# Split forms of the inner activations in 14 pieces between the product groups of the next up tiles

## Chip, cores and metric

The kernel runs on one core of one Trainium2 chip. The metric is the device time of one execution in microseconds (us), lower is better; every time below comes from runs of the kernel before or from the trace of one profiled execution of it.

## What is computed

The reference is one layer of a decoder trunk: four token mixers in parallel, an output projection, and a SwiGLU feed-forward block. The change touches the feed-forward block alone:

```python
h2 = layer_norm(x) * (1.0 + sc2) + sh2
up_a, up_b = jnp.split(h2 @ p['w_ffn_up'], 2, axis=-1)
ffn = (jax.nn.silu(up_a) * up_b) @ p['w_ffn_down']
x = layer_norm(ALPHA_DN * x + (1.0 + g2) * ffn, p['ln2_g'], p['ln2_b'])
```

There are 1056 tokens (1024 of the prompt, 32 of the samples), a model width of 1024 and an inner width of 2816, which is 22 tiles of 128. The inner activations are `silu(up_a) * up_b`.

## The kernel before

Tokens stand in three blocks of 352 (`TB`), the halves of a block are 176 wide (`HB`). Each matrix product is made in float16 from high and low halves, three matmuls for each product of 128 by 128 (`mm3`, L89).

**Seven products.** Most of the feed-forward block is computed by the scheme with seven products in place of eight (`seven`, L1655). Each tile of it is computed in two parts: a wide one of two blocks (matmuls of 352 columns) and a narrow one of one block (176 columns); `SUBS` lists them. So a tile has 14 product groups, in the order of `ORDER7` (L1653); a group is 12 matmuls for an up tile and 9 for a down tile. Products 0, 2, 3 and 5 are summed in the same PSUM bank, one after the other. After 0, 2 and 3 ScalarE (ACT) copies the bank's running sum out (L1683, to the tiles `ct`, `cu` or `af`), and TensorE (PE) can't begin product 2 before the copy after 0 is done, nor 3 before the copy after 2, nor 5 before the copy after 3. Products 1 and 6 share a second bank, product 4 has its own (`x7`). VectorE (DVE) adds the others (L1680). Below, "the copy after product 2" is the one of the wide part unless the narrow one is named, and "the work between" is what PE's order holds between the last matmul of product 2 and the first of product 3 of the wide part.

**Up tiles.** `up` makes one tile of inner activations, `af`, from h2: seven products, then tanh on ACT (L1854) and three steps on DVE (L1855, L1857). Tiles come in pairs; `ups(i)` makes tiles 2i and 2i+1. Pairs 0 and 1 are computed directly (L1820 to L1834), pairs 2 to 10 by seven products.

**Split forms.** Before a pair can be an input of the down projection, `forms(i)` makes seven combinations of its four quarters, each split in a high and a low half, in a slot of `ring` (3 slots, L1841). For each of the two parts there are 4 subtractions on DVE (L1869, in place in `af`), 7 high halves on ACT (L108) and 7 low halves on DVE (L116). A low half waits for its high half, a combined form for its subtraction.

**The order.** The loop at L1921 to L1934 is: forms 0, forms 1, up pair 2; forms 2, up pair 3; down chunk 0 (4 tiles, which read three slots); forms 3, up pair 4; forms 4, up pair 5; forms 5, up pair 6; down chunk 1; and again three pairs and down chunk 2. The tile framework puts the instructions of each engine into an order of its own: an instruction of a higher priority stream goes first where it is ready in the framework's model of time. `self.sup` (evacuations and weights) stands before `self.br` (the forms), which stands before `self.lo` (matmuls). Each engine's queue is then fixed and runs in order.

**Weights.** For each tile `pair_weights` (L1613) loads two blocks of weights by DMA (queue of SyncE), scales them on ACT (L1622), makes five sums on GpSimd (POOL: L1635 to L1643) and splits seven forms, high half on ACT (L1630), low half on POOL (L1631). The high and low halves are the tiles `whl` and `wf`.

## Time and profile before

| What | us |
|---|---|
| median of 3 runs | 1918.86 |
| lowest and highest run | 1918.74, 1921.48 |
| profiled execution, its own time | 1927.88 |
| its span, from the first to the last instruction | 1925.8 |
| PE busy, share of the span | 1734.6, 90% |
| DVE busy | 1297.0, 67% |
| ACT busy | 970.8, 50% |
| POOL busy | 953.9, 50% |

The seven-product part of the feed-forward block runs from 1282 to about 1840 us of the span. The profiled execution took 9.0 us longer than the median, so a difference worked out from its trace is carried over to the median as a difference. 2.1 us of its time lie outside the span.

### The profile page before, as it was taken

How to read it: one execution, taken by the hardware profiler on the slowest of the kernel's cores; microseconds unless marked ns; L12 is line 12 of the kernel's file. 1: busy time of each engine (PE TensorE's matmuls, PEld its weight loads, DVE VectorE, ACT ScalarE, POOL GpSimd, SP SyncE). 2: the span in 40 equal slices, each digit the busy share in tenths (PEclk: the TensorE clock that was granted, in tenths of full speed). 3: DMA queues.
4: the chain of work that ended last, by engine and by line, in shares of the span. 5: the costliest groups of instructions: out<-in, count | busy, mean ns of one | idle time of the engine just before them, and what ended most of it. 6: DMA issues, size and time to landing. Idle time of an engine off the chain costs nothing.

```text
span 1925.8 us, 36541 instructions
## 1 busy us (share of the span) xinstructions
PE 1734.6 (90%) x14985; PEld 1198.5 (62%) x14985; DVE 1297.0 (67%) x2161; ACT 970.8 (50%) x1796; POOL 953.9 (50%) x952
## 2 busy tenths in 40 slices
PE   7899999999899998788689899988999998999896
PEld 3466666656566665556367555556666776767675
DVE  6763777668676765386986479677467657755748
ACT  3642454465554645235664665645445644554434
POOL 1826421222354444744541553278577667675733
PEclk9999999999999999889799999989999999999999
DMA  8222220122311112313232340001121112111112
GB/s 310 75 90 64 73 59 23 49 58 54 96 50 58 62 40 98 73 41 102 77 110 77 129 137 1 1 23 44 48 64 56 48 44 65 56 37 53 50 28 91
DMA packets 63615, 130.60 MB, mean 68 GB/s; under 512 B 16408, under 2 KB 35928, under 8 KB 63192
## 3 DMA queue, kind: packets, MB, share of 16 engines
q1 hardware_dynamic: 61912, 124.07, 20.8%
q0 software_dynamic: 1536, 4.20, 0.7%
q8 instruction: 117, 1.92, 0.4%
q14 instruction: 50, 0.41, 0.1%
HBM read 117.36 MB, written 10.88 MB: 67 GB/s over the span
## 4 chain that ended last, share of the span: by engine, by line
PE 35%; DVE 26%; POOL 12%; ACT 10%; DMA 9%; issue 7%; SPq 1%; another core or an unknown queue 0%; ACTq 0%; DVEq 0%; POOLq 0%
PE gps L87 25%; DMA wraw<-in_w_up 3%; POOL wf L1631 2%; DVE x L1903 2%; POOL whl L1631 2%; DVE ring L116 2%; PE nps L87 1%; DMA wraw<-in_w_down 1%; DVE af L1869 1%; ACT wraw L1622 1%; DVE dacc L758 1%; POOL wraw L1635 1%; PE dp L87 1%; POOL wraw L1638 1%; POOL wraw L1639 1%
## 5 line engine op out<-in xcount | busy, mean ns | idle before, releaser
L87 PEld LDWEIGHTS <-whl 128*128 128x128 f16 x6992 | 623.5, 100 | 386.1 <-issue 74.9
L87 PE MATMUL gps<-h,whl 128*128 128x352 f16 (+1 forms) x4344 | 692.9, 314 | 49.0 <-ACT ct L1683 14.8
L87 PEld LDWEIGHTS <-wf 128*128 128x128 f16 x2232 | 197.7, 99 | 71.6 <-issue 13.8
L1631 POOL TENSOR_TENSOR wf<-wraw,wf 128x512 f16<-128x512 f32 (+1 forms) x102 | 122.8, 1206 | 145.8 <-ACT wf L1630 142.9
L1631 POOL TENSOR_TENSOR whl<-wraw,whl 128x512 f16<-128x512 f32 (+1 forms) x136 | 169.2, 1250 | 47.0 <-ACT whl L1630 46.8
L114 POOL TENSOR_TENSOR whl<-wraw,whl 128x1024 f16<-128x1024 f32 (+1 forms) x66 | 149.1, 2260 | 81.2 <-ACT whl L108 79.2
L105 ACT ACTIVATE wraw<-wraw 128x1024 f32<-128x1024 f32 (+2 forms) x96 | 96.4, 1005 | 127.4 <-DMA wraw<-in_w_gate 40.1
L87 PE MATMUL gps<-tf,whl 128*128 128x352 f16 (+1 forms) x1152 | 141.1, 280 | 18.6 <-ACT ct L1683 6.9
L1622 ACT ACTIVATE wraw<-wraw 128x1024 f32<-128x1024 f32 (+1 forms) x68 | 66.5, 978 | 111.0 <-DMA wraw<-in_w_up 62.2
L1630 ACT ACTIVATE whl<-wraw 128x512 f16<-128x512 f32 (+1 forms) x136 | 79.9, 589 | 78.8 <-POOL wraw L1635 34.5
L87 PE MATMUL gps<-ring,whl 128*128 128x352 f16 (+1 forms) x864 | 103.8, 276 | 13.1 <-DVE x L1903 13.1
L87 PE MATMUL gps<-y,wbr 128*128 128x352 f16 x576 | 105.4, 319 | 8.1 <-DVE gth L1771 3.8
L1680 DVE TENSOR_TENSOR ct<-ct,gps 128x352 f32<-128x352 f32 (+1 forms) x84 | 35.4, 424 | 106.5 <-PE gps L87 90.5
L1523 POOL TENSOR_TENSOR mix<-mix,gth 128x352 f32<-128x352 f32 x48 | 54.0, 1125 | 98.0 <-DVE gth L1494 87.1
L87 PE MATMUL gps<-mix,wo 128*128 128x352 f16 x576 | 88.8, 315 | 5.7 <-DVE gth L1771 3.4
L116 DVE TENSOR_TENSOR ring<-af,ring 128x352 f16<-128x352 f32 (+2 forms) x134 | 82.0, 645 | 7.8 <-ACT ring L108 7.7
L108 ACT ACTIVATE whl<-wraw 128x1024 f16<-128x1024 f32 (+1 forms) x82 | 84.8, 1035 | 4.4 <-DMA wraw<-in_w_ada 3.5
L87 PE MATMUL gps<-h,wf 128*128 128x352 f16 (+1 forms) x624 | 79.4, 283 | 6.6 <-DVE gth L1494 5.5
L87 PEld LDWEIGHTS <-wbr 128*128 128x128 f16 x576 | 56.5, 99 | 39.2 <-issue 10.2
L87 PEld LDWEIGHTS <-wo 128*128 128x128 f16 x576 | 56.7, 99 | 38.6 <-issue 5.9
L108 ACT ACTIVATE ring<-af 128x352 f16<-128x352 f32 (+2 forms) x134 | 52.2, 427 | 46.4 <-DVE af L1869 30.4
L87 PE MATMUL gps<-tf,wf 128*128 128x352 f16 (+1 forms) x528 | 66.6, 283 | 3.8 <-ACT cu L1683 3.6
(625 smaller groups left out, 3381.4 us busy)
## 6 DMA issues: line engine op xcount, KB each, us to landing
wraw<-in_w_up SPq DMA_DIRECT2D x44, 512.0 KB, 3.5
wraw<-in_w_gate SPq DMA_DIRECT2D x32, 512.0 KB, 3.9
wraw<-in_w_ada SPq DMA_DIRECT2D x32, 512.0 KB, 3.5
wraw<-in_w_in SPq DMA_DIRECT2D x20, 512.0 KB, 4.0
wraw<-in_w_down SPq DMA_DIRECT2D x24, 384.0 KB, 3.1
x<-in_xT SPq DMA_DIRECT2D x12, 704.0 KB, 7.7
araw<-in_w_ada SPq DMA_DIRECT2D x16, 512.0 KB, 10.9
wraw<-in_w_branch SPq DMA_DIRECT2D x8, 512.0 KB, 3.5
```

The source lines that it names most:

```text
L87: self.nc.tensor.matmul(out, lhsT=lhsT, rhs=rhs, start=start, stop=stop, skip_group_check=resume)
L105: nc.scalar.activation(src, src, AF.Copy, scale=scale)
L108: nc.scalar.activation(hi, src, AF.Copy, scale=scale)
L114: nc.gpsimd.tensor_tensor(lo, src, hi, op=ALU.subtract)
L116: nc.vector.tensor_tensor(lo, src, hi, op=ALU.subtract)
L758: nc.vector.scalar_tensor_tensor(acc[:, :L], ext[:, k:k + L], wts[:, i, k:k + 1], acc[:, :L], op0=ALU.mult, op1=ALU.add)
L1523: nc.gpsimd.tensor_tensor(o, o, g, op=ALU.add)
L1622: nc.scalar.activation(raw, raw, AF.Copy, scale=SW)
L1630: nc.scalar.activation(hi, src, AF.Copy)
L1631: nc.gpsimd.tensor_tensor(lo, src, hi, op=ALU.subtract)
L1680: add = lambda o, p: nc.vector.tensor_tensor(o, o, p, op=ALU.add)
L1903: nc.vector.scalar_tensor_tensor(x[:, h, z], part(h, z), gate[:, m, 0:1], x[:, h, z], op0=ALU.mult, op1=ALU.add)
```

## The change

`forms` no longer issues its instructions itself. It returns the slot and a generator with 14 steps (7 forms for the wide part, then 7 for the narrow one); each step is one form: its subtraction, where it has one, the high half and the low half. The order of the forms becomes 0, 1, 6, 3, 2, 4, 5. `seven` takes one step after each product group, while a generator is set, inside `issue_after(self.dve)`: each DVE instruction of the step is queued behind the DVE instruction noted last (an add, or the last step of an evacuation). ACT instructions of the step get no such edge. Only the last forms made before a pair are handed to it: forms 1 to pair 2, 2 to 3, and so on up to forms 8 to pair 9; forms 0 is made at once, as before. After the 14 groups of a pair's first tile all steps are taken.

```diff
+            def add(o, p):
+                self.dve = nc.vector.tensor_tensor(o, o, p, op=ALU.add).ins
...
+            if self.side is not None:
+                with self.tc.issue_after(self.dve):
+                    next(self.side, None)
...
-            for b, nb in self.SUBS:
...
-                with self.br:
-                    put(0, x1)
-                    sub(x1, x2, x1)
-                    put(1, x1)
-                    sub(x2, y2, x2)
-                    put(6, y2)
-                    sub(x1, y2, x1)
-                    put(2, x1)
-                    put(3, x2)
-                    put(4, y1)
-                    sub(y1, y1, x1)
-                    put(5, y1)
-            return R
+            def make():
+                for b, nb in self.SUBS:
...
+                    for f, src, p, q in ((0, x1, None, None), (1, x1, x2, x1), (6, y2, None, None), (3, x2, y2, x2),
+                                         (2, x1, y2, x1), (4, y1, None, None), (5, y1, y1, x1)):
+                        with self.br:
+                            if p is not None:
+                                sub(src, p, q)
+                            put(f, src)
+                        yield
+
+            return R, make()
...
-        def ups(i):
+        def ups(i, side=None):
+            self.side = side
             for t in (2 * i, 2 * i + 1):
                 w = self.full_forms()
                 self.pair_weights([I["w_up"][2 * t + j] for j in range(2)], 4, w)
                 up(t, w)
-
-
-        rs = [forms(i) for i in range(NSK // 2)]
+            for _ in self.side or ():
+                pass
+            self.side = None
+
+
+        rs = []
+        for i in range(NSK // 2):
+            R, side = forms(i)
+            rs.append(R)
+            if i < NSK // 2 - 1:
+                for _ in side:
+                    pass
         ahead = NSK // 2
-        ups(ahead)
+        ups(ahead, side)
```

No engine gets more or fewer instructions: DVE has 2163 in its order before and after, ACT 1798, PE 28936 (matmuls and weight loads). The order changes from the first forms on. Line numbers behind the edits shift: L1683 becomes L1685, L1869 becomes L1878, L1903 becomes L1908.

DVE, first tile of pair 4, right after the last down tile of chunk 0. Of before (`ring` is a low half, L1869 a subtraction, `x_13853` and `mod` belong to the down tile's evacuation, and the last row is the add of product 4, narrow part):

```order
L116 TENSOR_TENSOR ring<-af_14268,ring 128x352 x3
L116 TENSOR_TENSOR ring<-af_14268,ring 128x176
L1898 TENSOR_TENSOR ct<-ct,mod 128x32
L1903 SCALAR_TENSOR_TENSOR x_13853<-ct,mod,x_13853 128x144
L116 TENSOR_TENSOR ring<-af_14268,ring 128x176 x2
L1869 TENSOR_TENSOR af_14268<-af_14268 128x352
L1869 TENSOR_TENSOR af_14268<-af_14268 128x176
L1907 TENSOR_TENSOR x_13853<-x_13853,ct 128x32
L1869 TENSOR_TENSOR af_14268<-af_14268 128x352
```

The same place in the changed kernel:

```order
L116 TENSOR_TENSOR ring<-af_14268,ring 128x352 x3
L1903 TENSOR_TENSOR ct<-ct,mod 128x32
L1908 SCALAR_TENSOR_TENSOR x_13853<-ct,mod,x_13853 128x144
L1878 TENSOR_TENSOR af_14268<-af_14268 128x352
L1912 TENSOR_TENSOR x_13853<-x_13853,ct 128x32
L1878 TENSOR_TENSOR af_14268<-af_14268 128x352
L116 TENSOR_TENSOR ring<-af_14268,ring 128x352
L1878 TENSOR_TENSOR af_14268<-af_14268 128x352
L116 TENSOR_TENSOR ring<-af_14268,ring 128x352
L1681 TENSOR_TENSOR ct<-ct,x_16875 128x176
```

The narrow part's low halves, three of them, no longer stand ahead of the first wide subtraction; the narrow part as a whole comes later.

ACT at the same place. Of before (`wraw`, `whl` and `wf` are weights; the two `ct` rows are the copies after product 2, wide and narrow):

```order
L1622 ACTIVATE wraw<-wraw 128x1024
L1630 ACTIVATE wf<-wraw 128x512
L1630 ACTIVATE whl<-wraw 128x512
L108 ACTIVATE ring<-af_14268 128x352
L108 ACTIVATE ring<-af_14268 128x176
L1683 ACTIVATE ct<-gps 128x352
```

In the changed kernel:

```order
L1622 ACTIVATE wraw<-wraw 128x1024
L1630 ACTIVATE wf<-wraw 128x512
L1630 ACTIVATE whl<-wraw 128x512
L108 ACTIVATE ring<-af_14268 128x352
L1685 ACTIVATE ct<-gps 128x352
L108 ACTIVATE ring<-af_14268 128x352
```

One high half, not two, stands between the weights and the copy after product 2.

ACT, second tile of pair 5, from the narrow copy after product 0 to the wide copy after product 2. Of before:

```order
L1683 ACTIVATE ct<-gps 128x176
L108 ACTIVATE ring<-af_14268 128x352
L1630 ACTIVATE wf<-wraw 128x512
L108 ACTIVATE ring<-af_14268 128x176
L108 ACTIVATE ring<-af_14268 128x352
L1622 ACTIVATE wraw<-wraw 128x1024
L108 ACTIVATE ring<-af_14268 128x176
L1683 ACTIVATE ct<-gps 128x352
```

In the changed kernel:

```order
L1685 ACTIVATE ct<-gps 128x176
L108 ACTIVATE ring<-af_14268 128x352
L108 ACTIVATE ring<-af_14268 128x176
L108 ACTIVATE ring<-af 128x176
L1630 ACTIVATE wf<-wraw 128x512
L1622 ACTIVATE wraw<-wraw 128x1024
L1685 ACTIVATE ct<-gps 128x352
```

The high halves of subtracted forms of the next forms (the second `128x352` and the second `128x176`) are gone from there; the last narrow piece of forms 4 has come in.

The framework also places the matmuls of product 4 otherwise. PE's order between products 2 and 3 of the wide part holds, beside the 12 narrow matmuls of product 2, these matmuls of product 4 (narrow and wide):

| tile | before | changed |
|---|---|---|
| pair 3, first | 11 narrow, 12 wide, 4 wide of the next product 0 | 12 narrow, 7 wide |
| pair 3, second | 12 narrow, 9 wide | 10 narrow, 5 wide |
| pair 4, first | 7 narrow, 12 wide, 2 of the next product 0 | 12 narrow, 8 wide |
| pair 4, second | 12 narrow, 12 wide | 9 narrow, 12 wide, 1 of the next product 0 |
| pair 5, first | 12 narrow, 9 wide | 12 narrow, 3 wide |
| pair 5, second | 12 narrow, 12 wide | 12 narrow, 4 wide |
| pair 6, first | 12 narrow, 5 wide | 12 narrow, 12 wide |
| pair 7, first | 8 narrow, 12 wide | 12 narrow, 8 wide |
| pair 7, second | 12 narrow, 9 wide | 9 narrow, 12 wide, 1 of the next product 0 |
| pair 8, first | 12 narrow, 12 wide, 3 of the next product 0 | 12 narrow, 3 wide |
| pair 8, second | 12 narrow, 11 wide | 12 narrow, 4 wide |

The rest of them stand behind product 3 in both kernels. At the end of down chunk 0, ACT's order in the changed kernel has the scaling of weights L1622 ahead of the wide copy after product 3 of the last down tile; before, it stood behind it. In the first tile of pair 9, the weights' high half `whl` (L1630) that stood ahead of the wide copy after product 3 (to `cu`) now stands behind it.

## Rows read from the trace of the kernel before

**Rows 1.** The page, part 1: busy time of the engines.
```profile
PE 1734.6 (90%) x14985; PEld 1198.5 (62%) x14985; DVE 1297.0 (67%) x2161; ACT 970.8 (50%) x1796; POOL 953.9 (50%) x952
```
**Rows 2.** Waits of PE, 1280 to 1840 us: total, times, longest.
```profile
PE gps L87 <- ACT ct L1683: 21.7, 14, 5.8
PE gps L87 <- DVE x L1903: 16.6, 12, 1.9
PE gps L87 <- POOL whl L1631: 4.9, 2, 4.4
PE gps L87 <- ACT cu L1683: 4.2, 4, 1.9
```
**Rows 3.** PE in order of time, pairs 2 and 3: start, length, [idle before].
```profile
1295.26 3.68 PE L87 MATMUL gps<-tf,whl 128*128 128x352 f16 x12 [5.77 <-ACT ct L1683]
...
1307.60 3.24 PE L87 MATMUL gps<-h,whl 128*128 128x352 f16 x12 [3.12 <-ACT ct L1683]
...
1317.17 3.81 PE L87 MATMUL gps<-tf,whl 128*128 128x352 f16 x17 [4.44 <-POOL whl L1631]
1320.82 1.95 PE L87 MATMUL gps<-tf,wf 128*128 128x352 f16 x12
1322.61 0.31 PE L87 MATMUL gps<-h,wf 128*128 128x352 f16 x1
...
1352.86 4.58 PE L87 MATMUL gps<-h,whl 128*128 128x352 f16 x39 [1.88 <-ACT ct L1683]
...
1359.12 2.86 PE L87 MATMUL gps<-tf,wf 128*128 128x352 f16 x24 [1.68 <-ACT cu L1683]
```
**Rows 4.** PE in order of time, boundary after chunk 0, pairs 4 and 5.
```profile
1443.22 4.21 PE L87 MATMUL gps<-ring,wf 128*128 128x352 f16 x36
...
1458.62 4.73 PE L87 MATMUL gps<-h,whl 128*128 128x352 f16 x39 [1.43 <-ACT ct L1683]
...
1479.00 4.88 PE L87 MATMUL gps<-h,whl 128*128 128x352 f16 x39 [1.62 <-ACT ct L1683]
...
1497.84 2.86 PE L87 MATMUL gps<-h,whl 128*128 128x352 f16 x24 [0.23 <-ACT ct L1683]
...
1518.62 4.88 PE L87 MATMUL gps<-h,whl 128*128 128x352 f16 x39 [1.27 <-ACT ct L1683]
```
**Rows 5.** Busy time in a window of pair 2: length, PE, PEld, DVE, ACT, POOL, clock, DMA.
```profile
1305.00:1310.00 5.00, 2.40 (x9) 1.26 (x9) 5.00 (x14) 2.77 (x8) 0.43 (x2) 0.68 0.24 97
```
**Rows 6.** ACT in order of time, around the copies of pairs 4 and 5.
```profile
1457.48 0.74 ACT L108 ACTIVATE ring<-af 128x352 f16<-128x352 f32 x2 [3.69 <-DVE af L1869]
1458.13 0.44 ACT L1683 ACTIVATE ct<-gps 128x352 f32<-128x352 f32 x1
...
1516.54 0.50 ACT L108 ACTIVATE ring<-af 128x352 f16<-128x352 f32 x1 [2.58 <-DVE af L1869]
...
1518.13 0.44 ACT L1683 ACTIVATE ct<-gps 128x352 f32<-128x352 f32 x1
```
**Rows 7.** DVE in order of time: low halves in pair 2 and in pair 4.
```profile
1302.75 3.48 DVE L116 TENSOR_TENSOR ring<-af,ring 128x352 f16<-128x352 f32 x4
...
1452.57 3.56 DVE L116 TENSOR_TENSOR ring<-af,ring 128x352 f16<-128x352 f32 x4
```
**Rows 8.** Groups of the wide forms on DVE, by form, 1100 us to the end.
```profile
L116 DVE TENSOR_TENSOR ring<-af,ring 128x352 f16<-128x352 f32 x67 | 49.2, 743 | 6.1 <-ACT ring L108 6.1
L1869 DVE TENSOR_TENSOR af<-af 128x352 f32<-128x352 f32 x36 | 24.2, 684 | 0.1
```
**Rows 9.** POOL: one low half of weights in order of time, and its group on the page.
```profile
1309.91 7.21 POOL L1631 TENSOR_TENSOR whl<-wraw,whl 128x512 f16<-128x512 f32 x1 [4.57 <-ACT whl L1630]
...
L1631 POOL TENSOR_TENSOR whl<-wraw,whl 128x512 f16<-128x512 f32 (+1 forms) x136 | 169.2, 1250 | 47.0 <-ACT whl L1630 46.8
```
**Rows 10.** ACT in order of time at the end of down chunk 0.
```profile
1441.30 0.46 ACT L1683 ACTIVATE af<-gps 128x352 f32<-128x352 f32 x1 [1.60 <-PE gps L87]
1443.36 1.06 ACT L1622 ACTIVATE wraw<-wraw 128x1024 f32<-128x1024 f32 x1 [1.60 <-POOL wraw L1635]
```

More of the change, by code (lines that the diff above doesn't have):

```diff
@@ L1679, in seven @@
             c11, c12, c22 = c[i][0][:, 0], c[i][0][:, 1], c[i][1][:, c[i][1].shape[1] - 1]
-            add = lambda o, p: nc.vector.tensor_tensor(o, o, p, op=ALU.add)
+            def add(o, p):
+                self.dve = nc.vector.tensor_tensor(o, o, p, op=ALU.add).ins
             with self.sup:
@@ L1832, in ffn @@
                     nc.vector.scalar_tensor_tensor(o, o, 1.0, va, op0=ALU.add, op1=ALU.mult)
-                    nc.vector.scalar_tensor_tensor(o, o, c2, vb, op0=ALU.mult, op1=ALU.mult)
+                    self.dve = nc.vector.scalar_tensor_tensor(o, o, c2, vb, op0=ALU.mult, op1=ALU.mult).ins
             self.place7(h2, b, self.t3[b])
@@ L1856, in evac @@
                 for h in range(2):
-                    nc.vector.scalar_tensor_tensor(d[:, h], d[:, h], c2, other[b][h], op0=ALU.mult, op1=ALU.mult)
+                    self.dve = nc.vector.scalar_tensor_tensor(d[:, h], d[:, h], c2, other[b][h],
+                                                              op0=ALU.mult, op1=ALU.mult).ins
             self.seven(w, 4, xu, self.SUBS, evac, ct)
@@ L1864, in forms @@
             X, Y = af[2 * i], af[2 * i + 1]
-            for b, nb in self.SUBS:
-                c = slice(b * HB, (b + nb) * HB)
-                x1, x2, y1, y2 = X[:, 0, c], X[:, 1, c], Y[:, 0, c], Y[:, 1, c]
-                put = lambda f, src: self.split(R[:, f, 0, c], R[:, f, 1, c], src)
-                sub = lambda o, p, q: nc.vector.tensor_tensor(o, p, q, op=ALU.subtract)
-                with self.br:
-                    put(0, x1)
-                    sub(x1, x2, x1)
-                    put(1, x1)
-                    sub(x2, y2, x2)
-                    put(6, y2)
-                    sub(x1, y2, x1)
-                    put(2, x1)
-                    put(3, x2)
-                    put(4, y1)
-                    sub(y1, y1, x1)
-                    put(5, y1)
-            return R
+            def make():
+                for b, nb in self.SUBS:
+                    c = slice(b * HB, (b + nb) * HB)
+                    x1, x2, y1, y2 = X[:, 0, c], X[:, 1, c], Y[:, 0, c], Y[:, 1, c]
+                    put = lambda f, src: self.split(R[:, f, 0, c], R[:, f, 1, c], src)
+                    sub = lambda o, p, q: nc.vector.tensor_tensor(o, p, q, op=ALU.subtract)
+                    for f, src, p, q in ((0, x1, None, None), (1, x1, x2, x1), (6, y2, None, None), (3, x2, y2, x2),
[6 more added lines that the diff above has]
+            return R, make()
         gate = self.mod[:, 40:48]
@@ L1918, in ups @@
                 up(t, w)
-        rs = [forms(i) for i in range(NSK // 2)]
+            for _ in self.side or ():
[8 more added lines that the diff above has]
+                    pass
         ahead = NSK // 2
-        ups(ahead)
+        ups(ahead, side)
         for c in range(3):
             while len(rs) < 3:
-                rs.append(forms(ahead))
+                R, side = forms(ahead)
+                rs.append(R)
                 ahead += 1
-                ups(ahead)
+                ups(ahead, side)
             for mp in range(KD // 2):
@@ L2006, in build @@
     B.wraw_bufs, B.whl_bufs = 3, 4
+    B.side = None
     B.consts()
```

## Prediction

> **What bounds the kernel.** I read the page's busy times first. PE is busy for 1734.6 of 1925.8 us, DVE 67%, ACT and POOL 50% [rows 1], so time can only come from PE's idle time or from its clock. I then read PE's waits between 1280 and 1840 us, the only part in which the order changes [rows 2]. The reader is to see four releasers there. ACT's copies `ct` hold PE for 21.7 us in 14 waits, the copies `cu` for 4.2, a low half of weights on POOL for 4.9, and the down tiles' L1903 on DVE for 16.6. The last is an evacuation that the change does not touch. At most 21.7 + 4.2 + 4.9 = 30.8 us are within the change's reach.
>
> PE in order of time shows where they are. Pair 2 has the three long ones, 5.77, 3.12 and 4.44 [rows 3]; pairs 3 to 5 have some of 0.23 to 1.88 [rows 3, 4]; the other seven `ct` waits, in pairs 3 and 5 to 8, add 21.7 less the seven shown there (5.77, 3.12, 1.88, 1.43, 1.62, 0.23, 1.27), 6.4 us, about 0.9 each. After the long waits the clock was down as well: 12 wide matmuls took 3.24 us behind the wait of 3.12, and 12 of them later run in 1.95 [rows 3]; the granted clock in that window was 0.68, a mean of the two levels of 1.2 and 2.4 GHz [rows 5]. From the starts 1320.82 and 1322.61 a wide matmul at full clock is 1.79/12 = 0.149 us [rows 3], and I take a narrow one, with half the columns, at half of it, 0.075.
>
> **Why the copies are late.** PE cannot begin product 3 before ACT's copy after product 2. ACT is not busy then; it waits, in its order, behind a high half whose subtraction DVE has not reached. At 1457.48 ACT had waited 3.69 us for a subtraction, and the copy followed at 1458.13; at 1516.54 it had waited 2.58 us [rows 6]. DVE meanwhile was working off low halves: four in 3.56 us at 1452.57 [rows 7]. A wide low half costs 0.743 us and a wide subtraction 0.684 on the mean of its group [rows 8]. The change does not shorten these. It alters what stands ahead of the copies and how much of product 4 PE has to do until they come.
>
> **Pair 2.** Up to its first forms nothing moves, and the high halves ahead of the first copy are those of forms 0, made at once as before: 5.77 stays. For the wait of 3.12, two of the four low halves in the row of 3.48 us [rows 7] go behind a subtraction, which is worth 0 to 1.7 us (3.48/2) to the copy. I take 0.8, the middle, since most of forms 1 still lies dense there in DVE's order. The wait of 4.44 is for one low half of weights on POOL that took 7.21 us where its group has a mean of 1.25 [rows 9], while DVE was busy for all 5.00 us of the window and its 14 instructions [rows 5]. Its worth is 0 to 4.44; I take half, 2.2, because the spread takes part of DVE's work out of the 7 us but not all of it. This is a cause read from one coincidence of rows. The Trainium skill (SBUF — State Buffer, Who interferes with whom) says that a DVE instruction with two SBUF inputs contends with a GpSimd instruction that reads SBUF, and that who issues first holds the shared pair of ports for one whole instruction. By that rule POOL would be let in after the DVE instruction that it met; the row's 7.21 is longer than one such instruction, so rule and row do not fit unless the lock is lost again and again, and by the rule alone nothing would be gained at this place: the sum would be 2.2 and 0.5 (its clock) less, and the time about 1916.
>
> With shorter waits, half of the slow matmuls behind these two come back: (3.24 − 1.95)/2 = 0.6 behind the first, and for 17 at the second (3.81 − 17 × 0.149 = 1.3)/2, rounded down to 0.5. Bounds are 0 and 2.6. Pair 2: −0.8 − 2.2 − 1.1 = **−4.1**.
>
> **First tiles of pairs 3 to 9.** With one narrow high half fewer ahead of the copy and the first wide subtraction one low half earlier (3.56/4 = 0.9 [rows 7]), the copy comes some 1.1 us earlier; the high half I take at 0.2, below the 0.37 of one in the row of 0.74 x2 [rows 6], as two overlap. Against that PE has less to do until then, by the table of product 4. In pair 4: (5 × 0.075) − (4 + 2) × 0.149 = −0.5, so −1.1 + 0.5 = −0.6. In pair 7: less work by 0.3, −0.8. In pair 3 less work by 1.3 (9 wide fewer, one narrow more) eats the 1.1: 0; the wait of 1.68 for `cu` [rows 3] has the same L1622 ahead of it in both orders and stays. In pair 5, 0.9 less work (6 wide) on a wait of 0.23 [rows 4]: 0. Pair 6 has 1.0 more work but little wait: 0. Pair 8 has 1.8 less work where its wait is of another product: I add +0.4, between 0 and 1.8 − 1.1 = 0.7. In pair 9 the longest `cu` wait, 1.9 [rows 2], stands behind a weight split that waits for POOL and now follows the copy: −1.5, between 0 and −1.9. First tiles: **−2.5**.
>
> **Second tiles.** There the subtracted forms of the next pair leave the place ahead of the copy. That removes at least the 0.50 high half, at most the wait of 2.58 as well [rows 6]; the copy cannot come before product 2 ends and L1622 still stands there, so I take 0.6, near the lower end. Work between is less by 0.75 in pair 3, 8 × 0.149 = 1.2 in pair 5 and 1.05 in pair 8: 3.0 − 3 × 0.6 = +1.2. In pair 4, where 1.62 stands [rows 4], it is nearly unchanged: −0.5. In pair 7 it is 0.37 more: −1.0. Second tiles: **−0.3**.
>
> **Boundary after chunk 0.** ACT's L1622 now stands ahead of the wide copy after product 3. It waited for POOL until 1443.36 and took 1.06; the copy was made at 1441.30 before [rows 10]. PE goes on to the product behind that copy at 1443.22 without a wait [rows 4]. If L1622 lands when it did, the copy ends at 1443.36 + 1.06 + 0.46 = 1444.9, 1.7 after PE's need, less the 6 matmuls of the next tile (some 0.4 to 0.9 us at either width) that PE can take in between: **+1.3**, between 0 (L1622 earlier) and 1.7.
>
> **DMA and counts.** No instruction is added and no DMA moves to another queue, so there is no term there; SP's order matters only through L1622, priced above.
>
> **Sum.** −4.1 − 2.5 − 0.3 + 1.3 = −5.6 us against the profiled execution's 1927.88, which gives 1922.3. That execution was 9.0 above the median of 1918.86; carried over as a difference, the forecast is **1913.3**.
>
> **Rivals.**
>
> *Slower: PE runs out of work.* The copies come no earlier, since ACT queues behind whichever high half waits for DVE, while product 4 has moved behind product 3. Then each us of work lost lengthens a wait that is there already: 1.3 + 0.75 (pair 3), 0.5 (4), 0.9 + 1.2 (5), 0.3 (7), 1.05 (8) = 6.0, and 1.3 at the boundary: +7.3, 1926. It decides where copies come earlier by less than about 0.8 us. For it speaks that every late copy of [rows 6] has DVE as its releaser and that DVE's total is unchanged; against it that fewer low halves precede the subtractions.
>
> *No change.* Gains and losses of 1 us cancel, or POOL's 7.21 stays (−3.4 + 0.5 of clock, about −3 in all), or the change does less than it says: the edges bind DVE alone, the framework hoists ACT's high halves as before, and the orders differ little in pair 2. Sums from −3.8 to +3.8; 1918 as its middle.
>
> *All waits on copies go.* The `ct` waits without the first are 15.9, `cu` 4.2, POOL 4.9, clock 2.4: 27.4 us. Three quarters of it would be −20, 1899. For it speaks that ACT is idle for half of the span; against it that forms 1 stays dense in pair 2 and that PE has less work between.
>
> **How the numbers follow.** A difference of 0.2%, 3.8 us, is about what a measurement of this kernel can tell from no change. Forecast (−3.8 to −14) 0.38, all waits gone 0.08, no change 0.32, slower 0.22. Faster is 0.38 + 0.08 = 0.46. The forecast's own range follows from the bounds of its terms: 1905 to 1915. The whole range leaves out half of the slower case's tail beyond its price and most of the large gain: 1903 to 1926.
>
> **What would show it.** In the trace after: the wait of 5.77 unchanged, that of 3.12 near 2.3, the POOL row at 4 to 5 us in place of 7.21; `ct` waits at 16 to 18 in place of 21.7; L1903's waits still near 16.6; in pairs 5 and 8 the second tile's wait grown by 0.4 to 0.6; a new wait of about 1.3 before the product behind `af` at the end of chunk 0. The forecast is wrong if `ct` waits grow beyond 21.7 (then PE ran out of work), if POOL's long row stays and the time still falls (then it came from copies), or if new waits arise in the down tiles.

## The result, and the profile after

The changed kernel takes 1930.23 us at the median (21 runs, 1921.37 to 1936.32), the kernel before 1918.86 (21 runs, 1914.25 to 1921.91): 11.4 us slower, a ratio of 1.0059 with a 95% interval of 1.0046 to 1.0071. The forecast was 1913.3 in a range of 1903 to 1926.

The two profiled executions alone would not tell this. Their spans are 1925.8 and 1925.3 us: that of before lay 9.0 us above its median, that of the changed kernel (1927.24) 3.0 below. Up to the first long wait of PE both orders are the same, and there the changed kernel was already 10.5 us ahead (the wait begins at 1279.00, [rows 3] 1289.49). So the profiles have to be laid over each other at that wait. A second profile of the program before exists (the first run below, "without the edge"). From the product ahead of that wait to the last up pair, busy time by windows of that profile, and then of the changed kernel (length; PE, PEld, DVE, ACT, POOL busy; clock; DMA):

```profile
1277.50:1819.80 542.30, 494.52 (x4284) 373.92 (x4283) 356.77 (x638) 279.76 (x603) 382.45 (x325) 0.98 0.17 52
```

```profile
1274.10:1828.90 554.80, 499.60 (x4282) 375.88 (x4280) 378.77 (x638) 281.86 (x602) 375.62 (x325) 0.98 0.17 51
```

The same work takes 12.5 us longer; against the first profile of before, laid over at the same marks (543.60 us), it is 11.2. Of the 12.5, 5.1 are PE's own busy time (499.60 − 494.52). PE has the same matmuls, so that is clock: by windows of 5 us, length times the share missing from the full granted clock adds up to 8.5 us without the edge and to 13.6 in the changed kernel. The other 7.4 are idle time of PE. DVE is busy 22.0 us longer with the same 638 instructions, POOL 6.8 shorter.

The changed kernel's page, part 1 (against [rows 1]: DVE 1297.0 before):

```profile
PE 1729.7 (90%) x14985; PEld 1196.4 (62%) x14985; DVE 1322.3 (69%) x2161; ACT 973.2 (51%) x1796; POOL 948.1 (49%) x952
```

Its waits of PE, 1270 to 1840 us (total, times, longest), which answer to [rows 2]:

```profile
PE gps L87 <- ACT ct L1685: 29.5, 16, 5.5
PE gps L87 <- DVE x L1908: 17.1, 12, 1.9
PE gps L87 <- ACT cu L1685: 2.7, 4, 1.4
PE x L87 <- ACT ring L108: 2.3, 1, 2.3
PE gps L87 <- DVE ct L1681: 2.2, 1, 2.2
PE gps L87 <- ACT af L1685: 0.8, 2, 0.5
PE gps L87 <- POOL whl L1631: 0.4, 1, 0.4
```

POOL's wait of 4.4 is gone, `cu` is smaller, and `ct` has grown from 21.7 to 29.5. The growth is in the second tiles of the pairs. PE in order of time, changed kernel, second tiles of pairs 4, 5, 7, 8 and 9:

```profile
1468.81 4.80 PE L87 MATMUL gps<-h,whl 128*128 128x352 f16 x39 [2.42 <-ACT ct L1685]
...
1509.58 2.86 PE L87 MATMUL gps<-h,whl 128*128 128x352 f16 x24 [2.77 <-ACT ct L1685]
...
1657.79 6.48 PE L87 MATMUL gps<-h,whl 128*128 128x352 f16 x39 [2.40 <-ACT ct L1685]
...
1698.67 4.53 PE L87 MATMUL gps<-h,whl 128*128 128x352 f16 x24 [2.58 <-ACT ct L1685]
...
1743.41 1.92 PE L87 MATMUL gps<-h,whl 128*128 128x352 f16 x6 [3.47 <-ACT ct L1685]
```

With pair 6 (1.46) these are 15.1 us in pairs 4 to 9, where the profile without the edge has 6.3 (1.51, 1.28, 1.37, 0.87, 1.30). First tiles of the same pairs wait 5.0 for `ct` and nothing for `cu`; without the edge 3.4 and 2.0.

Such a wait could grow because PE has less work until it needs the copy, or because the copy comes later. The end of product 6 of the first tile is a mark that both kernels have. PE of pair 5 (the end of the first row is the mark, the next row waits for the copy), without the edge:

```profile
1498.21 2.86 PE L87 MATMUL gps<-h,wf 128*128 128x352 f16 x24
...
1511.36 4.88 PE L87 MATMUL gps<-h,whl 128*128 128x352 f16 x39 [1.28 <-ACT ct L1685]
```

In the changed kernel, whose waiting row is the 2.77 above:

```profile
1494.93 2.86 PE L87 MATMUL gps<-h,wf 128*128 128x352 f16 x24
```

PE works for 9.0 us behind the mark in both, and goes on 10.3 us behind it without the edge, 11.8 with the change. In pairs 4, 7 and 8 it has 9.3, 9.3 and 9.0 us of work where it had 8.6, 8.3 and 8.6, and goes on at 11.7, 11.7 and 11.6 where it went on at 10.1, 9.7 and 10.7. So in these tiles the copy is later, and PE has no less to do. In pair 9 PE has more work, 7.7 us for 6.1, and waits 3.47 us where it did not wait. Only in pair 6 does it have less, 7.7 us for 8.7; there the copy too is later, begun 8.7 us behind the mark where it began 6.6 behind it.

Part of why such a copy is late shows on DVE at the end of a first tile. Without the edge (pair 5), DVE has finished the forms and stands idle for 4.61 us until PE ends product 6 (4.60 in the first profile of before):

```profile
1495.09 0.51 DVE L1681 TENSOR_TENSOR ct<-ct,x 128x352 f32<-128x352 f32 x1
1500.20 0.52 DVE L1681 TENSOR_TENSOR ct<-ct,gps 128x352 f32<-128x352 f32 x1 [4.61 <-PE gps L87]
```

In the changed kernel it is still at the narrow forms when product 6 is done, and the add of product 6, which begins the evacuation, goes straight behind them with no wait for PE:

```profile
1495.57 1.42 DVE L1878 TENSOR_TENSOR af<-af 128x176 f32<-128x176 f32 x1
...
1498.04 0.34 DVE L116 TENSOR_TENSOR ring<-af,ring 128x176 f16<-128x176 f32 x1 [0.16 <-ACT ring L108]
1498.30 0.76 DVE L1681 TENSOR_TENSOR ct<-ct,gps 128x352 f32<-128x352 f32 x2
```

The same holds for all six first tiles of pairs 4 to 9: no idle time of DVE ahead of this add, where there are 1.8 to 5.6 us without the edge. The evacuation's last step ends 9.3 us behind the mark of pair 5, where it ended 6.2 behind it. Not all of that is DVE: the tanh of this evacuation began at 1499.47, behind weight splits that stood in ACT's order behind a narrow high half, and that had waited 2.35 us for its subtraction. ACT, which has high halves of that tile in its order, then gets to the second tile's copy later (ACT, changed kernel, pair 5, second tile; its PE wait is the 2.77 above):

```profile
1506.15 0.35 ACT L108 ACTIVATE ring<-af 128x176 f16<-128x176 f32 x1 [2.04 <-DVE af L1863]
1507.37 0.35 ACT L108 ACTIVATE ring<-af 128x176 f16<-128x176 f32 x1 [0.87 <-DVE af L1878]
...
1508.14 1.04 ACT L1622 ACTIVATE wraw<-wraw 128x1024 f32<-128x1024 f32 x1
1509.09 0.44 ACT L1685 ACTIVATE ct<-gps 128x352 f32<-128x352 f32 x1
```

The clock by windows of the changed kernel, around the waits of 2.42, 2.40 and 2.58 (columns as above):

```profile
1465.00:1470.00 5.00, 2.58 (x18) 1.56 (x16) 2.44 (x5) 2.71 (x6) 2.38 (x3) 1.00 0.35 112
...
1655.00:1660.00 5.00, 2.60 (x12) 1.36 (x11) 1.42 (x4) 3.64 (x7) 1.36 (x2) 0.81 0.36 108
...
1700.00:1705.00 5.00, 5.00 (x33) 3.45 (x32) 1.38 (x3) 2.08 (x4) 0.37 (x1) 0.75 0.18 68
```

Behind 2.40 and 2.58 part of the matmuls ran at the lower of the two levels, behind 2.42 none did. So the longer waits cost clock as well, though not each of them; the runs of the changed kernel spread over 15 us, those of before over 8.

### The profile page after: what moved, and what is told of

Same layout as the page of the kernel before. It is cut to its first block, busy times and chain, and to the rows that moved or that the text cites. A ratio compares the mean times of both kernels' runs of the same rounds, so it can differ in the third digit from the quotient of the medians.

```text
span 1925.3 us, 36536 instructions
## 1 busy us (share of the span) xinstructions
PE 1729.7 (90%) x14985; PEld 1196.4 (62%) x14985; DVE 1322.3 (69%) x2161; ACT 973.2 (51%) x1796; POOL 948.1 (49%) x952
## 4 chain that ended last, share of the span: by engine, by line
PE 31%; DVE 28%; ACT 12%; DMA 11%; POOL 11%; issue 7%; SPq 1%; ACTq 0%; another core or an unknown queue 0%; DVEq 0%; POOLq 0%
PE gps L87 22%; DMA wraw<-in_w_up 3%; DMA wraw<-in_w_down 3%; POOL wf L1631 2%; DVE ring L116 2%; DVE af L1878 2%; DMA wraw<-in_w_gate 2%; DVE x L1908 2%; ACT wraw L1622 1%; POOL whl L1631 1%; PE nps L87 1%; DVE dacc L758 1%; POOL whl L114 1%; DVE af L1861 1%; ACT wf L1630 1%
## 5 line engine op out<-in xcount | busy, mean ns | idle before, releaser
L1631 POOL TENSOR_TENSOR whl<-wraw,whl 128x512 f16<-128x512 f32 (+1 forms) x136 | 162.8, 1202 | 57.2 <-ACT whl L1630 56.8
L1622 ACT ACTIVATE wraw<-wraw 128x1024 f32<-128x1024 f32 (+1 forms) x68 | 66.5, 979 | 103.5 <-DMA wraw<-in_w_up 52.0
L1630 ACT ACTIVATE whl<-wraw 128x512 f16<-128x512 f32 (+1 forms) x136 | 79.7, 588 | 74.4 <-POOL wraw L1635 31.5
L1630 ACT ACTIVATE wf<-wraw 128x512 f16<-128x512 f32 (+1 forms) x102 | 59.1, 584 | 18.3 <-PE x L87 7.5
```

Source lines behind the costliest of these rows:

```text
L1622: nc.scalar.activation(raw, raw, AF.Copy, scale=SW)
L1630: nc.scalar.activation(hi, src, AF.Copy)
L1631: nc.gpsimd.tensor_tensor(lo, src, hi, op=ALU.subtract)
```

## The experiments

The ratios are to runs of the kernel before that were timed together with each run, with their 95% intervals. `side` is the generator of a pair's 14 steps.

**Without the edge.**

```diff
-                with self.tc.issue_after(self.dve):
-                    next(self.side, None)
+                next(self.side, None)
```

> The changed kernel without the edge alone: the 14 steps and their new order of forms stay, but no instruction is queued behind a noted one. On all five engines the order then is row for row that of the kernel before. So every theory expects the time of before, 1916 to 1921 us; the run shows that the whole loss hangs on the edge, and it is a second profile of the program before. Waits of PE on ct between 1280 and 1840 us should be 20 to 23 in total. If the POOL row of 7.21 us is made by DVE's dense work, it comes again at 6 to 8; if it was chance, that row is near 1.25 and the wait of 4.44 is gone.

1918.77 us, 1.0005 (0.9993 to 1.0017). The generator, its places and the new order of forms do nothing by themselves; the whole loss hangs on the edge. The waits on `ct` and `cu` come back to within 0.3 us one by one (21.2 and 4.0 in total). So does POOL's long row, in POOL's order of time:

```profile
1302.72 7.21 POOL L1631 TENSOR_TENSOR whl<-wraw,whl 128x512 f16<-128x512 f32 x1 [4.56 <-ACT whl L1630]
```

It is no chance: among the kernels with whole POOL instructions, 7.21 us stands in the five that leave DVE's dense run in pair 2 as it was, and in none of those that break it up.

**The last step moved, two steps at once, an edge on ACT too.** Three ways to get the steps out of the way of the second tile's copy.

```diff
-            if self.side is not None:
+            if self.side is not None and ((f, i) != (6, 1) if self.skip else (f, i) == (3, 1)):
...
         def ups(i, side=None):
-            self.side = side
             for t in (2 * i, 2 * i + 1):
+                self.skip = t % 2 == 0
+                self.side = side
```

> The changed kernel with the 14th step (the last narrow form, with a subtraction) not behind the first tile's last evacuation but in the second tile, behind the narrow product 3. PE's order stays that of the changed kernel in all second tiles but those of two pairs, where 0.15 us of work between products 2 and 3 is added. Theory E (a step tied behind the evacuation holds ACT, and with it the copy after product 2 of the second tile): the waits there, 2.42, 2.77, 1.46, 2.40, 2.58, 3.47, shrink by about 1.1 each (0.87 us wait for the subtraction and 0.25 for the high half), the time falls by 5 to 8, to 1922 to 1925. Theory F (less product-4 work between products 2 and 3 is the cause): the waits stay and the time stays at 1928 to 1932.

1932.01 us, 1.0075 (1.0056 to 1.0094). The waits of the second tiles did shrink in five pairs of six, to 1.58, 2.33, 1.62, 1.71, 2.21 and 1.60 in all, but those of first tiles grew (pair 3 from 2.86 to 3.77, pair 4 from 0.54 to 1.36), and `ct` came to 30.8.

```diff
-                    next(self.side, None)
+                    for _ in range(2 if f == 0 else 1):
+                        next(self.side, None)
```

> The changed kernel with two steps, not one, behind each of the first two product groups, so that all 14 are queued before the first tile's evacuations. Theory E (steps 13 and 14 stand between the steps of the evacuation on DVE, where one narrow instruction takes up to 1.3 us): evacuation and copies come some 2.5 us earlier, second tiles wait 0 to 1 us each, time 1915 to 1920. Theory F (work between): the waits of the second tiles follow that work, which is 2.72 in place of 3.54 us in pairs 4 and 7 (waits grow to 3.2), 4.53 in place of 2.42 in pairs 5 and 8 (waits fall to 0.5), 2.27 in place of 2.57 in pair 9 (3.8); in sum about -3 against the changed kernel, 1927.

1935.61 us, 1.0090 (1.0073 to 1.0108), the slowest with whole POOL instructions. Pairs 4 and 7 wait 1.43 in their second tiles, where theory F wanted 3.2; but pairs 5 and 8 now wait 3.87 for `cu`, and first tiles 1.28 to 2.48. Both theories fall: with all steps ahead of the evacuation the wait is in the first tile, and it is longer.

```diff
-                    nc.scalar.activation({0: c11, 2: c12, 3: c22}[f], ps, AF.Copy)
+                    self.act = nc.scalar.activation({0: c11, 2: c12, 3: c22}[f], ps, AF.Copy).ins
...
-                with self.tc.issue_after(self.dve):
+                with self.tc.issue_after(self.dve), self.tc.issue_after(self.act):
```

> The changed kernel with a second edge: ACT's high half of each step is queued behind the copy noted last, as DVE's part is behind the add noted last. Theory E in its wider form (high halves that ACT's order takes early, and which there wait for DVE, are what holds the copies): ct waits between 1280 and 1840 us fall from 29.5 to under 15, second tiles wait under 1 us, time 1910 to 1918. Theory F: second tiles of pairs 4 and 7 have 2.49 us of work between products 2 and 3 (3.54 in the changed kernel) and wait 3 us or more, pairs 5 and 8 have 4.53 and wait nothing; time 1925 to 1930.

1930.99 us, 1.0071 (1.0054 to 1.0087); `ct` 29.1. High halves floating on ACT are not the cause either. The waits here are those of theory F: 3.17 and 3.18 us in the second tiles of pairs 4 and 7, under 1 for the copies in those of pairs 5 and 8. In the run before it the same theory had been wrong, so the work between shapes where a wait falls, but not the total. Each run moved the wait, none took it away; DVE was the suspect that was left.

**POOL reads nothing.** In two kernels POOL's low halves of weights become a memset and its sums are left out.

```diff
-                nc.gpsimd.tensor_tensor(lo, src, hi, op=ALU.subtract)
+                nc.gpsimd.memset(lo, 0.0)
```

> The kernel without the edge, with POOL reading nothing in the part with seven products: its low halves of weights are replaced by a memset of the same tile, and its five sums of weights are left out. It is the base for the next run, and its time stands for itself. Theory G (DVE instructions with two inputs in SBUF wait for POOL's instructions): on DVE the narrow subtraction falls from a mean of 427 ns to about 330, and the wide low half from 734 to about 515, which is what the adds with an input in PSUM take. If they stay, G falls.

> The changed kernel with its edge, with the same left out of POOL's work. Theory G (the edge costs time because single DVE instructions queued between others meet POOL's instructions one by one): the narrow subtraction stays near 330 ns where it is 821 in the changed kernel, and the time is within 4 us of the run without the edge. Theory H (the order of waits alone: high halves on ACT that wait for DVE's queue, with copies behind them): the kernel with the edge is slower by 8 us or more here too.

1851.31 us without the edge (0.9651, 0.9633 to 0.9669), 1850.15 with it (0.9638, 0.9624 to 0.9652). All of PE's waits in this part, 1250 to 1747 us, without the edge:

```profile
PE gps L87 <- ACT ct L1681: 5.4, 2, 5.1
```

The narrow subtraction takes 334 and 337 ns, the wide low half 533 in both. With POOL's reads left out DVE has room to spare, and where it does the forms costs nothing. That DVE is near its limit is POOL's doing; whether the loss comes from longer DVE instructions is a different question, and these two runs don't answer it, since they remove all waits at once.

**Edge on the wide steps; pair 2 left out.**

```diff
-                with self.tc.issue_after(self.dve):
-                    next(self.side, None)
+                if self.taken < 7:
+                    with self.tc.issue_after(self.dve):
+                        next(self.side, None)
+                else:
+                    next(self.side, None)
+                self.taken += 1
```

> The changed kernel with the edge on the seven wide steps only; the seven narrow ones are taken at the same places without it. Theory G: the narrow subtractions, 821 ns on the mean in the changed kernel and 427 without any edge, come back to 430 to 500, most of the loss goes, time 1917 to 1923. Theory H: the wide steps hold the first tiles' copies as before, time 1925 to 1930.

1931.29 us, 1.0050 (1.0033 to 1.0066). The narrow subtractions did come back, to 377 ns, DVE's busy time too (355.28 us over the part laid over above), and the loss stayed: theory G falls as the cause of it, and so does any theory of the narrow steps behind the evacuation.

```diff
-            if i < NSK // 2 - 1:
-                for _ in side:
-                    pass
+            for _ in side:
+                pass
...
-        ups(ahead, side)
+        ups(ahead)
```

> The changed kernel with forms 1 made at once and nothing spread in pair 2. By the stage times pair 2 is where the change gained: 1.9 us lost up to the first copy to cu, then 5.5 gained up to the next pair's, with the wait of 4.44 us for a POOL low half gone. If that is so, the wait of 4.44 comes back, with a POOL row near 7.2 us, and the time is 2 to 5 us above the changed kernel, 1932 to 1935. If the gain there is paid for in pair 3, the time is that of the changed kernel or less.

1932.7 us, 1.0053 (1.0036 to 1.0069), not to be told from the changed kernel. POOL's row of 7.21 is back with a wait of 2.83; what pair 2 gains is too small to be seen in the time.

**Edge off, or on, forms 0 and 1.** The inputs of these two are there one tile earlier. Count on DVE, between the wide adds of product 6, the 22 instructions of the forms that end in the first tiles of pairs 5, 6, 8 and 9. Without the edge 6 stand in the second tile of the pair that they are made from, a head start, and 16 in the next first tile. In the changed kernel none has the head start: 19 stand in the next first tile, and the last 3, narrow ones, behind its add of product 6.

```diff
-                with self.tc.issue_after(self.dve):
+                if self.taken % 7 > 1:
+                    with self.tc.issue_after(self.dve):
+                        next(self.side, None)
+                else:
                     next(self.side, None)
+                self.taken += 1
```

> The changed kernel with the edge left off the steps of forms 0 and 1 (four of 14), whose inputs are there one tile earlier than the others'. Theory D (the edge takes from DVE the head start in the pair's own second tile and presses its work into the next first tile): these four go back to where they were, waits of the first tiles return to those without the edge, time 1917 to 1922. Theory G with the steps behind the evacuation as its place: narrow subtractions and low halves of the other forms stay where they are, time 1926 to 1931.

1920.24 us, 1.0002 (0.9991 to 1.0014): the time is that of the run without the edge, with 10 of 14 steps still tied. Not pair by pair: the waits for `ct` and `cu` in pairs 4 to 9 come to 14.3 us, against 11.7 without the edge and 20.1 in the changed kernel. Second tiles of pairs 4, 7 and 9 are relieved (1.47, 1.47 and 0.91), those of pairs 5 and 8 are not (2.95 and 3.01): there the narrow forms still stand right ahead of product 6's add. In the first tiles of pairs 5, 6, 8 and 9 DVE has no idle time ahead of that add here either, and the kernel as a whole loses nothing. On the other side POOL's wait of pair 2 stays gone. The narrow subtractions still take 626 ns, the wide low halves 811 (DVE's groups by form, 1270 to 1830 us, of this run; below them the narrow subtraction without the edge, and in the changed kernel):

```profile
L116 DVE TENSOR_TENSOR ring<-af,ring 128x352 f16<-128x352 f32 x65 | 51.1, 811 | 9.9 <-ACT ring L108 9.3
...
L1882 DVE TENSOR_TENSOR af<-af 128x176 f32<-128x176 f32 x36 | 22.0, 626 | 0.0
```

```profile
L1877 DVE TENSOR_TENSOR af<-af 128x176 f32<-128x176 f32 x36 | 15.1, 427 | 0.1
```

```profile
L1878 DVE TENSOR_TENSOR af<-af 128x176 f32<-128x176 f32 x36 | 29.5, 821 | 0.3
```

```diff
-                if self.taken % 7 > 1:
+                if self.taken < 2:
```

> The kernel without the edge, but with the edge on two of the 14 steps: the wide steps of forms 0 and 1. On DVE three instructions for each pair (two wide low halves and a subtraction) move from the second tile of the pair into the first tile of the next: of the 22 of a pair's forms 3 and 19 stand in second and first tiles, where they are 6 and 16 without any edge and 9 and 13 with the edge off these forms (with 3 of the 9 behind the first tile's evacuation). The narrow steps stay free. Theory D (the head start): this alone loses most of what the whole change loses, 1925 to 1932 us, with PE's waits on copies in the first tiles of pairs 5 and 8 grown from under 0.5 to 1.5 us or more. If the loss needs all 14 edges (narrow steps behind the evacuation, spacing), the time is 1917 to 1922.

1932.55 us, 1.0062 (1.0047 to 1.0076). Three DVE instructions for each pair, some 2 us by [rows 8], held back by one tile, lose as much as the whole change, although DVE's busy time is that of the run without the edge (358.47 us from 1276.9 to 1831.9, against 356.77). ACT, and then PE, of this run in the first tile of pair 5:

```profile
1487.36 0.35 ACT L108 ACTIVATE ring<-af 128x176 f16<-128x176 f32 x1 [1.30 <-DVE af L1882]
1487.62 1.04 ACT L1622 ACTIVATE wraw<-wraw 128x1024 f32<-128x1024 f32 x1
1488.57 0.48 ACT L108 ACTIVATE ring<-af 128x352 f16<-128x352 f32 x1
1488.95 0.44 ACT L1685 ACTIVATE ct<-gps 128x352 f32<-128x352 f32 x1
```

```profile
1489.45 2.86 PE L87 MATMUL gps<-h,whl 128*128 128x352 f16 x11 [2.08 <-ACT ct L1685]
```

From the narrow add of product 6 (1477.95) PE had work for 9.4 us, and the copy began 11.0 us behind it; without the edge (1481.91) work for 8.3 and the copy at 8.2. PE had more to do there, not less: it is the copy that comes 2.8 us later. It is not for want of idle time at the end of a first tile, which stays what it was or grows; DVE at the end of this tile:

```profile
1500.74 0.52 DVE L1681 TENSOR_TENSOR ct<-ct,gps 128x352 f32<-128x352 f32 x1 [5.61 <-PE gps L87]
```

Here the forms are late at the beginning of the first tile, and its own copies wait (2.08 and 1.77 us for `ct` in pairs 5 and 8, 2.66 and 2.86 for `cu` in pairs 6 and 9); in the changed kernel it is the second tiles' copies.

**POOL's instructions in halves.** The same arithmetic, each of POOL's weight instructions cut in two.

```diff
+            def two(e, o, p, q, op):
+                for z in (slice(0, kn // 2 + kn % 2), slice(kn // 2 + kn % 2, kn)):
+                    e.tensor_tensor(o[:, z], p[:, z], q[:, z], op=op)
...
-                nc.gpsimd.tensor_tensor(lo, src, hi, op=ALU.subtract)
+                two(nc.gpsimd, lo, src, hi, ALU.subtract)
...
-            eng.tensor_tensor(a22, a21, a22, op=ALU.add)
+            two(eng, a22, a21, a22, ALU.add)
```

The other sums are cut in the same way.

> The kernel without the edge, with every POOL instruction of the weights in the part with seven products (five sums and seven low halves for each tile) cut in two of half the columns. The arithmetic is the same. Theory G (a DVE instruction that meets a POOL instruction waits for the rest of it): the waits per meeting halve, DVE's busy time between 1280 and 1830 us falls by 20 us or more, time 1905 to 1916. Rival P (what counts is how long POOL needs for a tile's weights, and twice as many instructions cost more): POOL's busy time grows, time 1919 to 1930.

> The changed kernel with the same POOL instructions cut in two. Theory G: the narrow subtraction falls from a mean of 821 ns to about 600, and the edge costs 3 to 6 us against the run without it, where it costs 11 with whole instructions. Theory H (the order alone): the edge still costs 9 us or more.

1936.98 us without the edge, 1.0087 (1.0072 to 1.0101), and 1921.41 with it, 1.0005 (0.9996 to 1.0015). Over the same 638 instructions DVE's busy time fell by 16 us (from 356.77 to 340.68), less than theory G said, and not by its mechanism: the forms got no shorter (the narrow subtraction went from 427 to 516 ns, the wide low half from 734 to 743). POOL's busy time grew from 382.45 to 430.44, and the time went rival P's way, beyond its range. With the edge the narrow subtraction takes 604 ns, as theory G had said. And the edge gains 15.6 us on this base, which no theory had expected. So two more runs asked whether the count in first tiles decides here too:

> POOL's weight instructions cut in two, and the edge off the steps of forms 0 and 1. In DVE's order 13 of a pair's 22 instructions stand in first tiles (16 without the edge, which took 1937 with halves; 19 with the whole edge, 1921). Theory D (the fewer in first tiles, the better) holds with halves too only if this is the fastest of the three: under 1921, perhaps 1912 to 1918. If the gain of the edge with halves comes from the spacing of the narrow steps or from PE's order, which the edge changes too, this stands with the whole edge: 1919 to 1926.

> POOL's weight instructions cut in two, and the edge on the two wide steps of forms 0 and 1 alone: three more DVE instructions of a pair in first tiles (19), narrow steps free. Theory D with halves: slower than the run without the edge by 5 us or more, 1942 or above. If PE's order is what gains with halves: up to the second down chunk the work between products 2 and 3 is that of the kernel with the whole edge within 0.2 us in most tiles, behind it that of the one without; the time then lies between, 1925 to 1933.

1913.5 us, 0.9979 (0.9968 to 0.9989), and 1926.99, 1.0051 (1.0037 to 1.0066). The first is the only kernel here that does the whole work and beats the kernel before, by 0.2%. Its waits of PE, 1270 to 1840 us, and behind them the first row of the halves without the edge:

```profile
PE gps L87 <- ACT ct L1689: 24.9, 12, 7.7
PE gps L87 <- ACT cu L1689: 12.3, 12, 1.7
PE gps L87 <- ACT af L1689: 2.5, 4, 0.7
PE gps L87 <- DVE cu L1685: 1.2, 1, 1.2
```

```profile
PE gps L87 <- ACT ct L1689: 39.7, 19, 8.0
```

The waits on the down tiles' evacuation, 16.6 us in [rows 2], are gone from it, as they nearly are from the halves without the edge (0.9 us): that comes with the halves, not with the order of the forms. The second run contradicts the count as the only cause: more instructions in first tiles, and yet 10 us faster than its base. All of them together:

| edge on | head start | next first tile | behind it | whole POOL instructions | halves |
|---|---|---|---|---|---|
| steps 2 to 6 of each part | 6 | 13 | 3 | 1.0002 | 0.9979 |
| nothing | 6 | 16 | 0 | 1.0005 | 1.0087 |
| two wide steps | 3 | 19 | 0 | 1.0062 | 1.0051 |
| seven wide steps | 3 | 19 | 0 | 1.0050 | |
| all, but pair 2 | 0 | 19 | 3 | 1.0053 | |
| all (the change) | 0 | 19 | 3 | 1.0059 | 1.0005 |
| all, and ACT | 0 | 19 | 3 | 1.0071 | |
| all, last step later | 0 | 19 | 3 | 1.0075 | |
| all, two at once | 0 | 22 | 0 | 1.0090 | |

With whole instructions the time follows the count, in steps: 13 and 16 lose nothing, six variants with 19 lose 0.5 to 0.75%, 22 loses 0.9%. The two kernels that lose nothing are the two with the full head start. With halves it does not, but the fewest are the fastest again. PE's order also changes in each of these kernels (the two with the edge on wide steps alone share theirs), and with halves that is perhaps the cause of the difference between the rows. No run changed DVE's order from that of before and kept PE's, so how much of the loss goes through PE's order stays open; the places read above (second tiles of the changed kernel, pair 5 with two wide steps) show late copies, and outside pair 6 no less work of PE.

## Why the prediction was wrong

Point by point, by its own terms:

- *Pair 2, −4.1: mis-sized.* PE has the same work behind it when product 0 of pair 3 begins, without the edge and in the changed kernel:

```profile
1335.00 5.56 PE L87 MATMUL gps<-tf,whl 128*128 128x352 f16 x48
```

```profile
1330.61 5.56 PE L87 MATMUL gps<-tf,whl 128*128 128x352 f16 x48
```

From the start of the first long wait (1282.38 and 1279.00) that is 52.6 us without the edge and 51.6 in the changed kernel: −1.0. At the same row of pair 3's second tile (1357.77 and 1354.18) −0.2 is left. The wait of 5.77 stayed (5.52). POOL's row did shrink, further than to the 4 to 5 us foreseen: the longest low half of pair 2 now takes 2.82. But in place of 3.12 and 4.44 stand 2.30, 0.28, 1.40 and 2.19, on other releasers, which the prediction had not looked for. That fits the run without pair 2, in which the gain can't be seen.
- *First tiles, −2.5: mis-sized.* In pairs 3 to 9 `ct` and `cu` together went from 9.0 to 7.8 us. Pairs 4 and 7 gained 0.9 and 0.6, as forecast, and pair 9 its `cu` wait; pairs 5, 6 and 9 lost as much in new `ct` waits.
- *Second tiles, −0.3: this is the step that failed.* It came out at +8.8 (15.1 against 6.3). The text took the subtracted forms that leave the place ahead of the copy as a gain of 0.6 and stopped there. It did not follow them to where they went: into the next first tile on DVE. In [rows 8] their price stood ready, and DVE's idle time ahead of product 6's add, 4.60 us in pair 5, was the cover; the prediction never looked at it. In the changed kernel that cover is gone in all six first tiles, and the evacuation and the second tile's copy are late. The runs on forms 0 and 1 show that the loss hangs on these two forms: with the edge off them it is gone, with the edge on their wide steps alone it is all there. They also show that the cover is not the whole cause, since the first of these runs has lost it in four first tiles and the second has kept it: what counts in both is the head start.
- *Work between products 2 and 3.* The rival that ended slower, 1926 with a chance of 0.22, had the sign and nearly the size, but by luck, for another reason: behind the mark at product 6 PE has as much work or more in five of the six second tiles (in pair 6 1.0 us less, of a wait of 1.46). The prediction's own sign of that rival, `ct` beyond 21.7, came out (29.5) without it. Pairs 4 and 7, where that work is unchanged or more by the table of product 4, lost 0.9 and 1.0 in their second tiles too.
- *Boundary after chunk 0, +1.3: 0.* L1622 was done earlier (it began at 1430.84, and the copy behind it ended at 1432.26, ahead of PE's need at 1433.66). It was inside the stated bounds.
- *Clock.* The sum had −1.1; measured are +5.1 us of PE's busy time. The text priced the clock only where waits would shrink.
- *Length of DVE's instructions.* The prediction took DVE's total as unchanged; it grew by 22.0 us. That is not what costs the time, by the runs with the edge on wide steps, which lose as much at DVE's old busy time.

By places, all of PE's waits moved by −1.6 us in pair 2, −0.8 in pair 3, −0.8 in the first tiles of pairs 4 to 9 (half of it a wait on a DVE add), +8.8 in the second tiles and +1.9 in the down tiles. That is +7.5, the idle time of 7.4 measured between the two profiles; with the clock's 5.1 it is the 12.5.

## What to carry to other kernels

An instruction tied behind another is not only later itself: list what it now stands ahead of on its engine, and how much idle time that engine had there. An engine at 67% can have no room in the very tile in which its answer is waited for; the idle time just ahead of the instruction that releases others is one budget, and it is read from the trace. Work that could start early is another: here the loss came wherever a few instructions lost their head start, with that idle time or without it. Two profiled executions can hide a difference larger than the change: lay them over each other at the last point at which they do the same.

## What the hardware showed

POOL and DVE hold each other up far more than expected. With POOL reading nothing DVE's wide low halves take 533 ns where they take 734, the narrow subtraction 334 in place of 427, and the kernel 69.0 us less (1851.31 against 1920.26; part of that is POOL's own work, which was left out). Adds with one input in PSUM don't gain: 515 and 332 ns with POOL's reads, 521 and 336 without. This agrees with the Trainium skill (SBUF — State Buffer, Who interferes with whom), where a DVE instruction with two SBUF inputs contends with a GpSimd instruction that reads SBUF, not with one that only writes it. That one of the two is blocked for a whole instruction does not describe POOL's row of 7.21 us, which stands in each of the five kernels that keep DVE's dense run.

The traces show what does. During that row (without the edge, from 1302.72 to 1309.93) DVE goes through 18 instructions with two SBUF inputs, each straight behind the other, at 0.33 or 0.51 us, their lengths with POOL silent. Then comes an add with an input in PSUM. POOL's row ends 1.1 us behind the start of that add, and it is DVE's next two instructions that are long, 0.86 and 1.47:

```profile
1308.83 0.51 DVE L1681 TENSOR_TENSOR cu<-cu,gps 128x352 f32<-128x352 f32 x1
1309.27 2.25 DVE L116 TENSOR_TENSOR ring<-af,ring 128x176 f16<-128x176 f32 x2
```

The ten kernels with whole POOL instructions have 17 POOL rows of over 2 us between 1285 and 1830 us. In 15 the row ends 0.85 to 1.11 us behind the start of the first DVE instruction with an input in PSUM, in two 1.0 behind the start of an idle time of DVE of 0.59. So in these traces POOL does not get in between DVE's instructions with two SBUF inputs while they follow each other without a break. This is read from coincidence in time; no run changed it on purpose. It would explain both sides of the change: dense forms make POOL wait, and forms spread out one by one wait for POOL (the narrow subtraction 821 ns in place of 427, DVE 22.0 us more, POOL 6.8 less).
